# A two-block network on one core: attention heads among late projections, a two-pass last key tile, a new recurrence order, and the closing norm in columns

## Chip, core and metric

The kernel runs on one core of a Trainium2 chip. A core has five engines with an in-order queue each: TensorE (PE in the profile; its weight loads are PEld), VectorE (DVE), ScalarE (ACT), GpSimd (POOL) and SyncE (SP, which only issues DMAs here). The metric is the device time of one execution in microseconds (us).

## The reference

A sequence of 512 tokens of width 1024 goes through a first block with two layers and then a second block with gated linear attention. The change touches the first layer's recurrence, the second layer's attention and the norm at the very end:

```python
# layer 0: recurrence
gate, xr = split(h @ w_in, 2); gate = gelu(gate)
xc = conv_b + sum(xpad[:, k:k + S] * conv_w[k] for k in range(4))
r, i = sigmoid(xb @ w_a + b_a), sigmoid(xb @ w_x + b_x)      # blocks of 256
log_a = -8 * r * softplus(-lam);  a = exp(log_a)
u = sqrt(-expm1(2 * log_a)) * (i * xc)
y = (scan of h = a * h + u) * gate;  return y @ w_out

# layer 1: attention over keys that an index picks
q, c, qi, ki, wi = split(h @ w_in);  c = rms_norm(c)
q_lat = q @ w_uk * ATT_SCALE                                  # 16 heads
score = sum(wi * relu(qi @ ki))          # 8 index heads, causal
idx = top_k(score, 128)
logits = q_lat @ c_sel + rel_bias[t5_bucket(dist)]
p = softmax(logits);  o = (p @ c_sel) @ w_uv;  return o @ w_o

# end of the second block
return x * rsqrt(mean(x * x) + EPS) * norm_final
```

## The kernel before

**Products.** Activations and weights lie feature by token, 128 features on the partitions. Each fp32 operand is split into a rounded part and the rest (`h`/`l`, type fp32r), and a product is made as three: h·h, l·h, h·l. `group()` issues these three for each k tile (L349 to L351), and `lin()` makes a 128x512 output tile from 8 k tiles, so from 24 products. The other products on TensorE are transposes and some in fp32 or bf16.

**Weights.** `Weights` (L222) loads weights in the fixed order of `weight_plan()` (L100), 3 chunks of 128x1024 ahead of use: a DMA on SP's queue, a copy to `wh` on ScalarE (L252), and the rest `wl` on VectorE or, for some keys, on GpSimd (L253).

**Jobs.** Work is written as jobs, lists of stages. `run(jobs)` issues, in step n, stage 0 of job n and then the later stages of the jobs before it. Each engine's instructions stand in its queue in about this order; the framework's scheduler moves some by their readiness. PSUM has 8 buffers that are taken in turn.

**Layer 0.** Eight jobs `conv_job` project `xr` (24 products each) and convolve it: eviction on VectorE, taps, split on ScalarE and VectorE (`split`, L362). Four jobs `recur_job` (key "ax") make gates from two blocks `xr` each: 4 small groups of products, tanh (L568), exp, tanh, square root (L590) on ScalarE, whose function tables are loaded anew when the function's set changes, and factors and a scan on VectorE. Eight `rgate_job` project the gate (24 products), apply gelu and multiply by the scan. The order is xr0 to xr3; xr4, xr5, ax0; xr6, xr7, ax1; gates 0, 1, ax2; gates 2, 3, ax3; gates 4 to 7. `bias_job` (L624) makes the table of the relative biases by one product, copies it (`biasrow`, L639, VectorE) and stores it in DRAM; it stands after gates 0, 1 and ax2. Then `rout` projects back, four tiles together and then four more.

**Attention.** 8 index heads score the keys of query tiles 1 to 3 (`index_job`, relu L784, sum L793). `select()` (L801) finds the 128 largest of each row: 16 rounds of `max` (L811) and `match_replace` (L812) on VectorE for each of the three tiles, and a mask after each (L814). Rounds are issued by `more()` in the heads' jobs, two in each of the first 16. There are 32 head jobs (`head_job`, L903), pair 0 for query tiles 0 and 1 (masks 0 and 1), then pair 1 for tiles 2 and 3 (masks 2 and 3), 16 each. A head loads its bias rows, makes logits (L927 to L929), the softmax (minimum with bias on VectorE L938, exponential L941 on ScalarE, reciprocal of the sums L943, scaling on GpSimd L946), transposes (L958), copies and splits the transposed probabilities (`pTh` L961, `pTl` L962, `pTf` L966), and multiplies by the values (L978, L979, and L981 in fp32 for the last key tile). Of every two heads one output pair is put together: two copies `olo` on ScalarE (L985, L986), two additions on VectorE (L987, L988), and the split (`oh` L993, `ol` L994). The jobs' order is the projections q0 to q7 among the index heads, 8 key tiles, the values among the first four heads, then the other heads.

**The end.** The last layer's tiles are made in a left and a right half of 256 tokens (`last_job`, addition L1453; squares `sq`, L1429 and L1433). `norm_job` (L1460) makes, per half, the sum over all features with two fp32 products with a matrix of ones (`tot`, L1467), root and reciprocal on 128x256 (L1471, L1472), and four products `fin` (L1477) with a DMA each (L1478).

Of the kernel before, what the change touches and what calls it, by code (L numbers as in the profile page):

```python
# [11 lines left out]
F32 = mybir.dt.float32  # L12
# [86 lines left out]

def weight_plan():  # L100

    plan = []
    for step in range(8):
        plan += [("xr" if step < 4 else "rgate", 2 * step % 8 + i) for i in range(2)]
        if 2 <= step <= 5:
            plan += [("ax", step - 2)]
    plan += [("routk", kk) for kk in range(4)] + [("rout", j) for j in range(4, 8)]
    plan += mlp_plan(0, HID_GROUPS, False)
    plan += [("att", j) for j in (0, 1, 2, 3, 4, 6, 7, 8, 9, 5, 10, 11, 12, 13)] + [("uk",), ("uv",)]
# [113 lines left out]
class Weights:  # L223
# [3 lines left out]
    def __init__(self, nc, wall, pool, ahead):  # L227
        self.nc, self.wall, self.pool, self.ahead = nc, wall, pool, ahead
        self.plan = weight_plan()
        self.done = []  # L230
        self.off = 0
        self.at = 0

# [14 lines left out]
    def _split(self, key, st, h, l, a, b):  # L248


        eng = self.nc.gpsimd if key[0] in ("att", "uk", "uv", "lr", "k", "dec") or key == ("q", 0) else self.nc.vector
# [3 lines left out]
    def fetch(self, n):  # L255
        while len(self.done) < min(len(self.plan), n):
# [23 lines left out]
def build(ctx, tc, xT, wall, par, relb, onehot, edges, out):  # L280
# [364 lines left out]
    for step in range(8):  # L645
        jobs += [(conv_job if step < 4 else rgate_job)(2 * step % 8 + i) for i in range(2)]
        if 2 <= step <= 5:
            jobs.append(recur_job(step - 2))
        if step == 4:
            jobs.append(bias_job())  # L650
# [20 lines left out]
    run([residual_job(j, lambda j=j: rout(j), nxt) for j in range(KD)])  # L671
# [98 lines left out]
    def index_job(i, h):  # L770
# [10 lines left out]
        def relu():  # L781

            d = st["d"] = T(name="dots") if on_pool else st["ps"]
# [119 lines left out]
    def head_job(pair, h):  # L903
# [5 lines left out]
        def loads():  # L909
# [38 lines left out]
        def transpose():  # L948
            probs = st["p"]
            st["pT"] = []  # L950
            for k0 in range(0, nfull + 1, 2):
# [7 lines left out]
                nf = 256 if k0 + 1 == nfull else 512  # L959
# [3 lines left out]
                pf = None  # L963
                if nf == 256:
                    pf = T(name="pTf")
                    act(pf[:, :P], ps[:, 256:256 + P], AF.Copy)  # L966
                st["pT"].append((ph, pl, pf))

        def values():
# [4 lines left out]
            for kt in range(nfull + 1):  # L974
                ph, pl, pf = st["pT"][kt // 2]
                if kt < nfull:
                    c = slice((kt % 2) * 256, (kt % 2) * 256 + 256)
                    PE.matmul(osl, value(kt, h), ph[:, c], start=kt == 0, stop=False)  # L978
                    PE.matmul(osl, value(kt, h), pl[:, c], start=False, stop=False)  # L979
                else:  # L980
                    PE.matmul(osl[:, P:], value(kt, h).bitcast(F32), pf[:, :P], start=False, stop=True)  # L981
# [3 lines left out]
            act(lo[0:64, :256], ops[64:128, 0:256], AF.Copy)  # L985
            act(lo[64:128, :256], ops[0:64, 256:512], AF.Copy)  # L986
            V.tensor_add(reverse(lo[0:64, 256:512]), blocks(lo[0:64, :256]), blocks(ops[0:64, 0:256]))  # L987
            V.tensor_add(reverse(lo[64:128, 256:512]), blocks(lo[64:128, :256]), blocks(ops[64:128, 256:512]))  # L988
# [4 lines left out]
            act(oh_[:, c], lo[:, 256:512], AF.Copy)  # L993
            G.tensor_sub(ol_[:, c], lo[:, 256:512], oh_[:, c].bitcast(F32))  # L994
# [11 lines left out]
    for j in range(1, 8):  # L1006
        jobs.append(q_job(j))
        if j == 3:
# [3 lines left out]
        if 3 <= j <= 5:  # L1012
            jobs.append([lambda: None, lambda j=j: copies(0, j - 3)])
        if 5 <= j <= 6:
            jobs.append([lambda: None, lambda j=j: queries(0, j - 5)])
    heads = [head_job(pair, h) for pair in range(2) for h in range(16)]

# [532 lines left out]
```

## Time and profile before

| | |
|---|---|
| median of 3 runs (lowest to highest) | 1905.28 us (1903.79 to 1905.71) |
| the profiled execution's own time | 1903.61 us |
| its span in the trace | 1901.8 us |
| busy: TensorE, VectorE, ScalarE, GpSimd | 1848.7, 1020.3, 813.4, 181.7 us |
| idle TensorE in the span | 53 us |

The trace gives every instruction's start and busy time. The start of one product to the start of the next is TensorE's pace; a product's busy time is longer, since products overlap in the pipeline. A number in brackets behind an instruction is the idle time before it on its engine, and who ended it. The granted clock is a share of TensorE's full 2.4 GHz: at 0.5 it runs at 1.2 GHz.

### The profile page before, as it was taken

What the parts mean: (1) busy time and instruction counts of PE and PEld (TensorE: products, weight loads), DVE (VectorE), ACT (ScalarE), POOL (GpSimd) and SP (SyncE); (2) the same over time, 40 slices, a digit from 0 to 9 for tenths busy, and PEclk for the clock granted to TensorE, in tenths of its full rate; (3) what the DMA queues carried; (4) which work ended last, traced back from release to release, by engine and by line L of the source; (5) the groups of instructions that cost most, each with busy time, mean ns of one, the idle gap of its engine ahead of it and who ended that gap; (6) DMA issues with size and microseconds to landing.
All of it is one profiled execution on the core that took longest, in us unless ns stands there. A gap on an engine that the chain in (4) does not pass through costs nothing.

```text
span 1901.8 us, 21845 instructions
## 1 busy us (share of the span) xinstructions
PE 1848.7 (97%) x8434; PEld 1526.0 (80%) x8434; DVE 1020.3 (54%) x1512; ACT 813.4 (43%) x1271; POOL 181.7 (10%) x194
## 2 busy tenths in 40 slices
PE   8989999999999679999999999999999999999997
PEld 6868888888878468888888888888888888888886
DVE  7886543344349956654244445735584554344345
ACT  6784432333244577443234445446543333132223
POOL 0000000000155264000000014211000000000000
PEclk9999999999999899999999999999999999999998
DMA  5222222222222530322222222231122222222221
GB/s 197 84 86 92 100 98 91 100 100 96 93 100 90 146 89 21 111 93 96 100 100 92 97 100 86 92 111 45 67 89 100 100 89 100 100 95 94 100 80 53
DMA packets 61000, 179.36 MB, mean 94 GB/s; under 512 B 7696, under 2 KB 18144, under 8 KB 60896
## 3 DMA queue, kind: packets, MB, share of 16 engines
q1 hardware_dynamic: 60752, 177.97, 27.6%
q8 instruction: 66, 1.08, 0.2%
q14 instruction: 38, 0.31, 0.0%
q10 hardware_dynamic: 144, 0.00, 0.0%
HBM read 168.48 MB, written 2.12 MB: 90 GB/s over the span
## 4 chain that ended last, share of the span: by engine, by line
PE 63%; DVE 4%; ACT 2%; issue 1%; DMA 0%; POOL 0%; SPq 0%; DVEq 0%; ACTq 0%
PE ps L349 14%; PE ps L351 13%; PE ps L350 13%; PE dn L350 5%; PE dn L351 5%; PE dn L349 5%; PE o L1319 1%; DVE score L812 1%; PE v L1225 1%; PE v L1224 1%; PE v L1226 1%; DVE top L811 1%; ACT probs L941 1%; PE kv L1293 1%; PE tot L376 0%
## 5 line engine op out<-in xcount | busy, mean ns | idle before, releaser
L252 ACT ACTIVATE wh<-wst 128x1024 fp32r<-128x1024 f32 (+2 forms) x314 | 328.2, 1047 | 910.3 <-PE ps L350 358.7
L349 PE MATMUL ps<-xh,wh 128*128 128x512 f32 x1376 | 542.5, 394 | 6.4 <-DVE biasrow L639 4.6
L351 PE MATMUL ps<-xh,wl 128*128 128x512 f32 x1376 | 536.6, 390 | 0.0
L350 PE MATMUL ps<-xl,wh 128*128 128x512 f32 x1376 | 536.5, 390 | 0.0
L253 DVE TENSOR_TENSOR wl<-wst,wh 128x1024 fp32r<-128x1024 f32 (+2 forms) x291 | 352.4, 1212 | 224.3 <-ACT wh L252 197.2
L349 PEld LDWEIGHTS ps<-xh,wh 128*128 128x128 f32 x1376 | 259.3, 188 | 62.8 <-issue 7.2
L350 PEld LDWEIGHTS ps<-xl,wh 128*128 128x128 f32 x1376 | 259.3, 188 | 56.3 <-issue 2.4
L351 PEld LDWEIGHTS ps<-xh,wl 128*128 128x128 f32 x1376 | 259.1, 188 | 54.1
L349 PE MATMUL dn<-h,wh 128*128 128x512 f32 (+1 forms) x712 | 271.7, 382 | 0.0
L350 PE MATMUL dn<-l,wh 128*128 128x512 f32 (+1 forms) x712 | 271.7, 382 | 0.0
L351 PE MATMUL dn<-h,wl 128*128 128x512 f32 (+1 forms) x712 | 271.7, 382 | 0.0
L350 PEld LDWEIGHTS dn<-l,wh 128*128 128x128 f32 x712 | 133.8, 188 | 26.0
L349 PEld LDWEIGHTS dn<-h,wh 128*128 128x128 f32 x712 | 133.8, 188 | 26.0
L351 PEld LDWEIGHTS dn<-h,wl 128*128 128x128 f32 x712 | 133.8, 188 | 25.8
L253 POOL TENSOR_TENSOR wl<-wst,wh 128x1024 fp32r<-128x1024 f32 x23 | 55.2, 2405 | 934.7 <-ACT wh L252 934.5
L422 DVE TENSOR_TENSOR x<-x,dn 128x512 f32<-128x512 f32 x48 | 33.0, 687 | 170.8 <-PE dn L351 170.8
L453 DVE SCALAR_TENSOR_TENSOR relu<-ps,std 128x512 f32<-128x512 f32 x64 | 44.2, 691 | 146.7 <-PE ps L351 146.6
L349 PE MATMUL ps<-h,wh 128*128 128x512 f32 x200 | 78.7, 396 | 5.5 <-ACT h L362 3.5
L350 PE MATMUL ps<-l,wh 128*128 128x512 f32 x200 | 77.8, 389 | 0.0
L351 PE MATMUL ps<-h,wl 128*128 128x512 f32 x200 | 77.8, 389 | 0.0
L349 PEld LDWEIGHTS ps<-h,wh 128*128 128x128 f32 x200 | 37.9, 190 | 15.1 <-ACT h L362 4.0
L1497 DVE TENSOR_TENSOR u<-ps,std 128x512 f32<-128x512 f32 x22 | 15.2, 690 | 62.5 <-PE ps L351 62.5
(315 smaller groups left out, 2129.2 us busy)
## 6 DMA issues: line engine op xcount, KB each, us to landing
wst<-wall SPq DMA_DIRECT2D x300, 512.0 KB, 3.2
btile<-biasdram SPq DMA_DIRECT2D x32, 128.0 KB, 3.0
qd<-qq SPq DMA_DIRECT2D x64, 64.0 KB, 2.1
wst<-wall SPq DMA_DIRECT2D x8, 384.0 KB, 3.0
x<-xT SPq DMA_DIRECT2D x8, 256.0 KB, 4.9
out_dram<-fin SPq DMA_DIRECT2D x8, 256.0 KB, 2.3
wst<-wall SPq DMA_DIRECT2D x6, 256.0 KB, 5.0
kto<-kth SPq DMA_DIRECT2D x8, 128.0 KB, 2.7
```

The lines of the kernel that those rows point to most:

```text
L252: self.nc.scalar.activation(h[:, a:b], st[:, a:b], AF.Copy)
L253: eng.tensor_sub(l[:, a:b], st[:, a:b], h[:, a:b].bitcast(F32))
L349: PE.matmul(ps, wh, xh, start=i == 0, stop=False)
L350: PE.matmul(ps, wh, xl, start=False, stop=False)
L351: PE.matmul(ps, wl, xh, start=False, stop=i == n - 1)
L422: V.tensor_add(xs[j], xs[j], st["ps"])
L453: stt(t, st["ps"], 0.0, feed.r, op0=ALU.max, op1=ALU.mult)
L811: V.max(top, acc[:, :w])
L812: V.match_replace(acc[:, :w], top, acc[:, :w], MARK)
L941: act(s[:, :w], s[:, :w], AF.Exp, scale=-1.0, bias=nm, accum_out=sums[:, a:a + 1])
L1224: PE.matmul(st["ps"][i], xh, hk, start=kt == 0, stop=False)
L1225: PE.matmul(st["ps"][i], xh, lk, start=False, stop=False)
```

## The change

Layer 0's jobs and weights get one order, `LAYER0`: seven projections, then the first recurrence, and the rest with one or two gate projections between recurrences. `bias_job` moves behind the first four output tiles. In attention the weights of q6 and q7 come after `uk` and `uv`; the output projection's weights ("wo") are held back until a job `further` behind head 9, and their `wl` is made on GpSimd; the first heads stand among q6, q7, the key tiles and the values; a head fetches the copies 3 pairs ahead and the queries 2 ahead; index head jobs of tile 1 write their relu to SBUF. The last key tile's probabilities are split with the others, and multiplied in two rounded passes. An output pair has one copy of 128x512. At the end the sums over the features are made as columns (128x2), root and reciprocal work on these, and two products with the identity spread them back into PSUM (`r`); the left half's norm is one job earlier.

```diff
+LAYER0 = ([("xr", j) for j in range(7)] + [("ax", 0), ("xr", 7), ("rgate", 0), ("ax", 1), ("rgate", 1), ("rgate", 2)]
+          + [("ax", 2), ("rgate", 3), ("rgate", 4), ("ax", 3)] + [("rgate", j) for j in range(5, 8)])
...
-    plan += [("att", j) for j in (0, 1, 2, 3, 4, 6, 7, 8, 9, 5, 10, 11, 12, 13)] + [("uk",), ("uv",)]
+    plan += [("att", j) for j in (0, 1, 2, 3, 4, 6, 7, 8, 9, 5, 10, 11)] + [("uk",), ("uv",), ("att", 12), ("att", 13)]
...
+        self.limit = self.plan.index(("wo", 0))
...
-        eng = self.nc.gpsimd if key[0] in ("att", "uk", "uv", "lr", "k", "dec") or key == ("q", 0) else self.nc.vector
+        eng = self.nc.gpsimd if key[0] in ("att", "uk", "uv", "wo", "lr", "k", "dec") or key == ("q", 0) else self.nc.vector
...
-        while len(self.done) < min(len(self.plan), n):
+        while len(self.done) < min(self.limit, n):
...
+    jobs += [{"xr": conv_job, "ax": recur_job, "rgate": rgate_job}[n](j) for n, j in LAYER0]
     run(jobs)
...
-    run([residual_job(j, lambda j=j: rout(j), nxt) for j in range(KD)])
+    jobs = [residual_job(j, lambda j=j: rout(j), nxt) for j in range(KD)]
+    run(jobs[:4] + [bias_job()] + jobs[4:])
...
-            d = st["d"] = T(name="dots") if on_pool else st["ps"]
+            d = st["d"] = T(name="dots") if on_pool or i == 1 else st["ps"]
...
-            if e == 0 and 1 <= n < 14:
-                copies((n + 2) // 8, (n + 2) % 8)
-            if e == 1 and 1 <= n < 15:
-                queries((n + 1) // 8, (n + 1) % 8)
+            if e == 0 and n + 3 < 16:
+                copies((n + 3) // 8, (n + 3) % 8)
+            if e == 1 and n + 2 < 16:
+                queries((n + 2) // 8, (n + 2) % 8)
...
-                nf = 256 if k0 + 1 == nfull else 512
+                nf = 384 if k0 + 1 == nfull else 512
...
-                pf = None
-                if nf == 256:
-                    pf = T(name="pTf")
-                    act(pf[:, :P], ps[:, 256:256 + P], AF.Copy)
-                st["pT"].append((ph, pl, pf))
+                st["pT"].append((ph, pl))
...
-                    PE.matmul(osl[:, P:], value(kt, h).bitcast(F32), pf[:, :P], start=False, stop=True)
+                ph, pl = st["pT"][kt // 2]
+                c = slice((kt % 2) * 256, (kt % 2) * 256 + (256 if kt < nfull else P))
+                dst = osl if kt < nfull else osl[:, P:]
+                PE.matmul(dst, value(kt, h), ph[:, c], start=kt == 0, stop=False)
+                PE.matmul(dst, value(kt, h), pl[:, c], start=False, stop=kt == nfull)
...
-            act(lo[0:64, :256], ops[64:128, 0:256], AF.Copy)
-            act(lo[64:128, :256], ops[0:64, 256:512], AF.Copy)
+            act(lo, ops, AF.Copy)
+            os_ = T(name="os")
+            V.tensor_add(reverse(os_[0:64, :256]), blocks(lo[64:128, 0:256]), blocks(ops[0:64, 0:256]))
+            V.tensor_add(reverse(os_[64:128, :256]), blocks(lo[0:64, 256:512]), blocks(ops[64:128, 256:512]))
...
-    for j in range(1, 8):
+    for j in range(1, 6):
         jobs.append(q_job(j))
...
+    jobs += kts[:2] + vals[:2] + [heads[0], q_job(6), heads[1], q_job(7)]
+    for i in range(2, 8, 2):
+        jobs += [heads[i // 2 + 1]] + kts[i:i + 2] + vals[i:i + 2]
+
+    def further():
+        W.limit = len(W.plan)
+        W.fetch(W.at + W.ahead)
+
+    run(jobs + heads[5:10] + [[further]] + heads[10:])
...
-            ps = st["ps"] = PS("tot")[:, :w]
-            for i in range(2):
-                PE.matmul(ps, ones, acc2[i][:, c], start=i == 0, stop=i == 1)
+            ps = st["ps"] = PS("tot")
+            for n in range(w // P):
+                cols = slice(c.start + n * P, c.start + (n + 1) * P)
+                for i in range(2):
+                    PE.matmul(ps[:, n:n + 1], acc2[i][:, cols], ones[:, 0:1], start=i == 0, stop=i == 1)
...
-            r = st["r"] = T(name="std")[:, :w]
-            act(r, st["ps"], AF.Sqrt, scale=1.0 / D, bias=eps_t)
-            V.reciprocal(r, r)
+            col = small(w // P, "rstd")
+            act(col, st["ps"][:, :w // P], AF.Sqrt, scale=1.0 / D, bias=eps_t)
+            V.reciprocal(col, col)
+            st["r"] = PS("r")[:, :w]
+            for n in range(w // P):
+                PE.matmul(st["r"][:, n * P:(n + 1) * P], col[:, n:n + 1].to_broadcast([P, P]), ident, start=True, stop=True)
...
-    jobs.insert(-2, norm_left[:3])
+    jobs.insert(-3, norm_left[:3])
```

TensorE's queue where the first recurrence's products (`ps_485` to `ps_506` from the split block `h_460` before, `ps_527` to `ps_548` after) follow the projections of `xr`; before:

```order
L350 MATMUL ps_435<-xl_189,wh_308 128x512
L351 MATMUL ps_435<-xh_188,wl_309 128x512
L349 MATMUL ps_485<-h_460,wh_340 128x512
L349 MATMUL ps_492<-h_460,wh_340 128x512
L349 MATMUL ps_499<-h_460,wh_340 128x512
L349 MATMUL ps_506<-h_460,wh_340 128x512
L349 MATMUL ps_530<-xh_148,wh_382 128x512
L350 MATMUL ps_530<-xl_149,wh_382 128x512
```

and now:

```order
L351 MATMUL ps_485<-xh_188,wh_340 128x512
L352 MATMUL ps_485<-xl_189,wh_340 128x512
L353 MATMUL ps_485<-xh_188,wl_341 128x512
L351 MATMUL ps_527<-h_460,wh_382 128x512
L351 MATMUL ps_534<-h_460,wh_382 128x512
L351 MATMUL ps_541<-h_460,wh_382 128x512
L351 MATMUL ps_548<-h_460,wh_382 128x512
L351 MATMUL ps_572<-xh_148,wh_430 128x512
```

One more projection, xr6 (now `ps_485`; `ps_435` before was xr5), stands ahead of the recurrence's first products.

VectorE's queue around the third mask (`mask3`); `probs` and `negmax` are a head's softmax minima, `sums` its reciprocals, `olo` and `os` an output pair's additions, `top` and `score` the selection's rounds. Before:

```order
L938 ISA probs_4996,negmax_4997<-logit_4976,btile_3784 128x128
L938 ISA negmax_4997 128x1
L938 ISA probs_5000,negmax_5001<-logit_4976,btile_3784 128x256
L938 ISA negmax_5001 128x1
L814 TENSOR_SCALAR mask3_3775<-score_4301 128x512
L943 RECIPROCAL sums_4964<-sums_4964 128x2
L987 TENSOR_TENSOR olo_5022<-olo_5022,o_4920 64x2x128
L988 TENSOR_TENSOR olo_5022<-olo_5022,o_4920 64x2x128
L943 RECIPROCAL sums_4995<-sums_4995 128x2
```

and now:

```order
L979 TENSOR_TENSOR os_5177<-olo_5175,o_5004 64x2x128
L980 TENSOR_TENSOR os_5177<-olo_5175,o_5004 64x2x128
L809 MAX top_5155<-score_4314 128x8
L810 MATCH_REPLACE score_4314<-top_5155,score_4314 128x512
L960 TENSOR_TENSOR pTl_5189<-pT_5184,pTh_5188 128x384
L936 ISA probs_5193,negmax_5194<-logit_5158,btile_3784 128x128
L936 ISA negmax_5194 128x1
L936 ISA probs_5197,negmax_5198<-logit_5158,btile_3784 128x256
L936 ISA negmax_5198 128x1
L812 TENSOR_SCALAR mask3_3775<-score_4314 128x512
L960 TENSOR_TENSOR pTl_5226<-pT_5221,pTh_5225 128x384
```

Ahead of the mask stood 7 heads' minima and one output pair; now stand 11 heads' minima, 8 splits `pTl` and 3 output pairs, and the last round of selection follows the third pair.

VectorE's queue at the end (`x` are the additions of the last layer, right half; `fin` the left half's closing products, then `sq` the right half's squares). Before:

```order
L1472 RECIPROCAL std_14255<-std_14255 128x256
L1453 TENSOR_TENSOR x_83<-x_83,dn_14232 128x256
L1477 TENSOR_TENSOR fin_14096<-fin_14096,std_14255 128x512
L1477 TENSOR_TENSOR fin_14032<-fin_14032,std_14255 128x512
L1477 TENSOR_TENSOR fin_14148<-fin_14148,std_14255 128x512
L1477 TENSOR_TENSOR fin_14197<-fin_14197,std_14255 128x512
L1433 TENSOR_TENSOR sq_14030<-sq_14030,sq_14282 128x256
L1453 TENSOR_TENSOR x_84<-x_84,dn_14258 128x256
L1429 TENSOR_TENSOR sq_14288<-x_84 128x256
L1472 RECIPROCAL std_14298<-std_14298 128x256
```

and now:

```order
L1473 RECIPROCAL rstd_14209<-rstd_14209 128x2
L1451 TENSOR_TENSOR x_82<-x_82,dn_14185 128x256
L1481 TENSOR_TENSOR fin_14072<-fin_14072,r_14212 128x512
L1481 TENSOR_TENSOR fin_14008<-fin_14008,r_14212 128x512
L1481 TENSOR_TENSOR fin_14124<-fin_14124,r_14212 128x512
L1481 TENSOR_TENSOR fin_14173<-fin_14173,r_14212 128x512
L1431 TENSOR_TENSOR sq_14006<-sq_14006,sq_14258 128x256
L1451 TENSOR_TENSOR x_83<-x_83,dn_14215 128x256
L1431 TENSOR_TENSOR sq_14006<-sq_14006,sq_14263 128x256
L1451 TENSOR_TENSOR x_84<-x_84,dn_14239 128x256
L1427 TENSOR_TENSOR sq_14269<-x_84 128x256
L1473 RECIPROCAL rstd_14281<-rstd_14281 128x2
```

The left half's four closing products stood after the addition of `x_83` and just before that of `x_84`; now they stand before both.

## Rows read from the trace of the kernel before

**Rows 1.** The page: busy time of each engine, share of the span, instructions.
```profile
PE 1848.7 (97%) x8434; PEld 1526.0 (80%) x8434; DVE 1020.3 (54%) x1512; ACT 813.4 (43%) x1271; POOL 181.7 (10%) x194
```

**Rows 2.** Busy us (instructions) by stretch; PEclk is the granted clock.
```profile
41.60:121.00 79.40, 69.28 (x293) 55.60 (x293) 67.72 (x93) 63.61 (x87) 0.00 (x0) 0.97 0.23 81
45.10:48.30 3.20, 3.15 (x8) 2.49 (x9) 3.20 (x6) 1.97 (x3) 0.00 (x0) 0.51 0.47 164
120.40:124.00 3.60, 3.58 (x10) 2.89 (x11) 3.60 (x6) 3.06 (x4) 0.00 (x0) 0.59 0.29 83
580.00:664.00 84.00, 65.92 (x296) 51.36 (x294) 81.97 (x206) 39.19 (x92) 29.90 (x29) 0.90 0.44 124
664.00:745.00 81.00, 70.05 (x435) 57.54 (x435) 55.51 (x192) 68.59 (x216) 50.49 (x77) 0.96 0.28 67
```

**Rows 3.** What TensorE waited for, 20 to 145 us: total, times, longest.
```profile
PE ps L349 <- DVE biasrow L639: 4.6, 1, 4.6
PE ps L349 <- ACT h L362: 3.5, 1, 3.5
PE ps L349 <- ACT rg L568: 2.0, 2, 1.1
```

**Rows 4.** Timeline of TensorE, layer 0: start, busy us, instruction, [idle before, releaser].
```profile
24.24 0.39 PE L349 MATMUL ps<-xh,wh 128*128 128x512 f32 x1
24.47 0.39 PE L350 MATMUL ps<-xl,wh 128*128 128x512 f32 x1
```

**Rows 5.** Timeline of VectorE around the third mask and the pairs' additions.
```profile
661.87 0.42 DVE L938 CUSTOM_DVE_ANT_0 probs<-logit,btile 128x256 f32<-128x256 f32 x1
...
662.21 1.43 DVE L814 TENSOR_SCALAR mask<-score 128x512 bf16<-128x512 f32 x1
...
663.64 0.39 DVE L987 TENSOR_TENSOR olo<-olo,o 64x256 f32<-64x256 f32 x1
...
667.72 0.17 DVE L943 RECIPROCAL sums<-sums 128x2 f32<-128x2 f32 x1 [1.42 <-ACT probs L941]
...
678.34 0.41 DVE L987 TENSOR_TENSOR olo<-olo,o 64x256 f32<-64x256 f32 x1 [0.62 <-ACT olo L986]
```

**Rows 6.** Timeline of ScalarE around a function table's load in layer 0.
```profile
91.31 1.28 ACT L590 ACT_TABLE_LOAD   x1
92.60 0.63 ACT L590 ACTIVATE rg<-rg 128x512 f32<-128x512 f32 x1
```

**Rows 7.** Groups by shape, 555 to 760 us: busy, mean ns, idle before.
```profile
L962 DVE TENSOR_TENSOR pTl<-pT,pTh 128x256 fp32r<-128x256 f32 x32 | 13.5, 421 | 5.0 <-ACT pTh L961 3.0 <-POOL probs L946 0.9
...
L253 DVE TENSOR_TENSOR wl<-wst,wh 128x1024 fp32r<-128x1024 f32 x4 | 5.2, 1292 | 0.0
...
L966 ACT ACTIVATE pTf<-pT 128x128 f32<-128x128 f32 x32 | 8.8, 276 | 9.9 <-DVE pTl L962 9.2 <-POOL ol L994 0.6
```

**Rows 8.** Timeline of TensorE in the values of pair 1.
```profile
714.82 0.28 PE L978 MATMUL o<-pTh,vv 128*128 128x256 f32 x1
714.94 0.28 PE L979 MATMUL o<-pTl,vv 128*128 128x256 f32 x1
...
715.82 0.39 PE L981 MATMUL o<-pTf,vv 128*128 128x128 f32 x2
716.04 0.38 PE L927 MATMUL logit<-mask,identb 128*128 128x512 bf16 x1
```

**Rows 9.** Timeline of TensorE and VectorE at the end.
```profile
1888.54 0.28 PE L351 MATMUL dn<-h,wl 128*128 128x256 f32 x1
...
1888.73 2.48 DVE L1477 TENSOR_TENSOR fin<-fin,std 128x512 f32<-128x512 f32 x4
...
1891.47 0.41 DVE L1453 TENSOR_TENSOR x<-x,dn 128x256 f32<-128x256 f32 x1
...
1894.22 1.75 DVE L1472 RECIPROCAL std<-std 128x256 f32<-128x256 f32 x1 [1.88 <-ACT std L1471]
```

**Rows 10.** What TensorE waited for, 620 to 745 us: the longest entry.
```profile
PE pT L958 <- POOL probs L946: 9.8, 4, 8.0
```

More of the change, by code (lines that the diff above doesn't have):

```diff
@@ L97, in mlp_plan @@
     return plan
+LAYER0 = ([("xr", j) for j in range(7)] + [("ax", 0), ("xr", 7), ("rgate", 0), ("ax", 1), ("rgate", 1), ("rgate", 2)]
+          + [("ax", 2), ("rgate", 3), ("rgate", 4), ("ax", 3)] + [("rgate", j) for j in range(5, 8)])
 def weight_plan():
[L102 to L106, printed above, removed]
+    plan = list(LAYER0)
     plan += [("routk", kk) for kk in range(4)] + [("rout", j) for j in range(4, 8)]
     plan += mlp_plan(0, HID_GROUPS, False)
-    plan += [("att", j) for j in (0, 1, 2, 3, 4, 6, 7, 8, 9, 5, 10, 11, 12, 13)] + [("uk",), ("uv",)]
+    plan += [("att", j) for j in (0, 1, 2, 3, 4, 6, 7, 8, 9, 5, 10, 11)] + [("uk",), ("uv",), ("att", 12), ("att", 13)]
     plan += [("wo", j) for j in range(8)]
@@ L644, in build @@
     jobs = [[lambda: None, softplus]]
[L645 to L650, printed above, removed]
+    jobs += [{"xr": conv_job, "ax": recur_job, "rgate": rgate_job}[n](j) for n, j in LAYER0]
     run(jobs)
@@ L974, in values @@
             for kt in range(nfull + 1):
[L975 to L980, printed above, removed]
-                    PE.matmul(osl[:, P:], value(kt, h).bitcast(F32), pf[:, :P], start=False, stop=True)
+                ph, pl = st["pT"][kt // 2]
[3 more added lines that the diff above has]
+                PE.matmul(dst, value(kt, h), pl[:, c], start=False, stop=kt == nfull)
             if e == 0:
@@ L992, in values @@
             c = slice(256 * pair, 256 * pair + 256)
-            act(oh_[:, c], lo[:, 256:512], AF.Copy)
-            G.tensor_sub(ol_[:, c], lo[:, 256:512], oh_[:, c].bitcast(F32))
+            act(oh_[:, c], os_[:, :256], AF.Copy)
+            G.tensor_sub(ol_[:, c], os_[:, :256], oh_[:, c].bitcast(F32))
         def more():
@@ L1005, in build @@
     jobs += [index_job(1, h) for h in range(8)]
-    for j in range(1, 8):
+    for j in range(1, 6):
         jobs.append(q_job(j))
+        if 3 <= j <= 5:
+            jobs.append([lambda: None, lambda j=j: copies(0, j - 3)])
+        if 4 <= j <= 5:
+            jobs.append([lambda: None, lambda: None, lambda j=j: queries(0, j - 4)])
         if j == 3:
@@ L1011, in build @@
             jobs += [index_job(2 + (j - 1) // 2, 4 * ((j - 1) % 2) + h) for h in range(4)]
[L1012 to L1015, printed above, removed]
     heads = [head_job(pair, h) for pair in range(2) for h in range(16)]
+    kts = [kt_job(j) for j in range(8)]
     vals = [v_job(kt, n) for kt, n in ((0, 0), (1, 0), (0, 1), (1, 1), (2, 0), (3, 0), (2, 1), (3, 1))]
-    first = []
-    for i in range(4):
-        first += [heads[i], vals[2 * i], vals[2 * i + 1]]
-    run(jobs + [kt_job(j) for j in range(8)] + first + heads[4:])
+    jobs += kts[:2] + vals[:2] + [heads[0], q_job(6), heads[1], q_job(7)]
[5 more added lines that the diff above has]
+    run(jobs + heads[5:10] + [[further]] + heads[10:])
     nxt = Feed("g_mlp1")
```

2 lines of the change are left out of this document (removed).

## The prediction

> **What bounds the kernel now.** I read first the busy shares: TensorE works 97% of the span [rows 1], so a change that leaves its products alone can win no more than its idle time, some 53 us, and what the products lose at a lower clock. Then the table by stretches, to find where that idle time lies in the stages that the change touches. In layer 0, from 41.60 to 121.00 us, TensorE stands 10.1 us (79.40 less 69.28), while VectorE has 67.72 us of work and ScalarE 63.61 [rows 2]. In attention, from 580 to 745 us, it stands 18.1 us of the first 84 and 10.9 of the next 81. VectorE is busy 81.97 of the 84 and only 55.51 of the 81 [rows 2]: the first stretch is VectorE's, the second nobody's. So two questions follow: which waits are the 10.1 us, and what makes VectorE full in one stretch and half idle in the next.
>
> The waits of layer 0 name three: 4.6 us for the bias row's copy, 3.5 us for the first split of a convolved block, and 2.0 for gates, together the window's 10.1 [rows 3]. Each long one leaves a cold stretch behind it: the granted clock is 0.51 for 3.20 us and 0.59 for 3.60 us [rows 2], so TensorE loses 3.20 x 0.49 = 1.57 us and 3.60 x 0.41 = 1.48 us there. A product of 512 columns follows the next after 0.23 us at the full clock [rows 4].
>
> In attention the third mask ends the selection at 662.21 [rows 5]: rounds of maximum and replacement on VectorE feed it, and the heads of pair 1 can't start before it. After it the pairs of pair 0 still unfinished are done, and then pair 1.
>
> **Layer 0, the order.** The seven projections now stand ahead of the first recurrence, so the block's split has 24 more products, 24 x 0.23 = 5.5 us of TensorE's work, to finish behind. That covers the 3.5 us wait and its 1.57 us of cold clock. One gate projection instead of two stands between some recurrences; a round there is 72 products, 16.5 us of TensorE. The bias product goes behind the first 28 products of the output projection, and its copy waits in VectorE's queue behind nothing that TensorE needs: 4.6 and 1.48 us go. With the 2.0 us for gates the most that can be had is 10.1 + 3.1 = 13.2 us. It costs one more function table on ScalarE, 1.28 us [rows 6]. If all is had, the window is 66.2 us, and must hold ScalarE's 63.61 + 1.28 = 64.9 us and VectorE's 67.7 us, of which the last scan and products can trail into the output projection. That is the edge, so I take 12 us, between 6 (only bias) and 13.2.
>
> The trace shows a table's load as one instruction of 1.28 us, and the work behind it starts 0.01 us after [rows 6]. The Trainium skill, page "ScalarE: Activation LUTs", section "What ACT_TABLE_LOAD costs", puts a drain of about 1.38 us beside the load, some 2.66 us a switch. By that, the eight loads in this window and the new one would hide up to 9 x 1.38 = 12.4 us more, and the gain here would be about 2 us. The row disagrees, and the sum goes by the row.
>
> **Attention, the order.** The first heads now start among the late q, k and v products. By the queue's order, VectorE does eleven heads' softmax minima ahead of the third mask instead of seven, and three output pairs instead of one; the fourth comes shortly after. So two pairs more are finished when pair 1 may begin. In the trace the second pair's additions start at 663.64 and the fourth's at 678.34 [rows 5]: 14.7 us. Not all of that is won, since the same instructions now stand before the mask, on the engine that is full there. The wider of a head's two minima takes 0.34 us to the next instruction (661.87 to 662.21), the narrower less, some 0.54 together [rows 5]: 2.2 for four heads. Four reciprocals of 0.17 and four additions of 0.4 are 0.7 and 1.6 [rows 5]; four splits of transposed probabilities 4 x 0.42 = 1.7 [rows 7]; that the eight splits there become half as wide again costs at most 8 x 0.21, and I estimate 0.9. Against that, four subtractions of the output projection's weights, 5.2 us [rows 7], leave VectorE for GpSimd; I count 4.6 of it, since busy times overlap those of the next instruction by a tenth or more. That nets 2.5 us. A split, two minima and a reciprocal of the fourth pair stay behind the mask, 1.4. 14.7 - 2.5 - 1.4 = 10.8 us.
>
> Two corrections. ScalarE loses a copy of 0.28 us for each head and chunk [rows 7], gets wider ones, and does one output copy for two: about 0.2 us for each of the remaining 12 pairs, where it is busy 68.59 of 81 us [rows 2]: +2. And heads in VectorE's in-order queue make it wait: today 2.03 us idle in the 84 [rows 2] over seven heads, 0.3 a head, so 3 us for eleven. Sum 10.8 + 2 - 3 = 10 us. The low end is 2, where VectorE waits for the heads longer; the high end 18, as VectorE's idle time over both stretches, 27.5 us [rows 2], is the most that any order could give and a third of it lies behind the last minima of a head.
>
> Index head 1's relu into SBUF instead of over its own PSUM frees a buffer and adds no instruction: nothing. The copies and queries of the heads are DMAs and splits moved one head or two earlier; SP's queue has fewer weight loads ahead of them, since the output weights are held back. Nothing, covered by the head before; the output weights come back with heads still to run.
>
> **Last key tile.** One fp32 product of 128 columns for each head and tile gives way to two rounded ones. The trace has the fp32 one at 0.22 us, two records together from 715.82 to 716.04 [rows 8]. It doesn't show a rounded one of 128 columns; the bounds are 0.06 each by the slope from 512 columns (0.23) to 256 (0.12) [rows 4, 8], so 0.13 for two, and 0.22 each if it is as slow per column as fp32. That is -0.09 to +0.22 a head. TensorE sets the end only for the 16 heads of pair 1: a gain of 1.4 to a loss of 3.5 us. I take 0, since the nearest row, 256 columns at 0.12, speaks for the lower half and the weight load behind each product for the other.
>
> **Closing norm.** The last product starts at 1888.54 and takes 0.28, but VectorE is in the left half's four closing products from 1888.73 for 2.48 us, and so the last addition waits until 1891.47 [rows 9]. In the new order these stand ahead of the last two additions, behind the left half's norm, which is one job earlier: the last addition can start at 1888.9, -2.6 us. Then the norm's root and reciprocal work on two columns instead of 256: the reciprocal of 128x256 takes 1.75 us [rows 9], one of 128x2 0.17 [rows 5]. The sums as columns are tiny products, and the spreading back costs two products of 128 columns, 0.22 each [rows 8] and a hop to TensorE and back. I take -1.7 in all. The left half's spreading now stands in TensorE's queue among the last products, and its chain of root and reciprocal may outlast the nine products ahead of it (9 x 0.12 = 1.1 us): +0.8. Sum: 3.5 us, between 1 and 5.
>
> **Sum.** 12 + 10 + 0 + 3.5 = 25.5 us. The profiled execution took 1903.61 us, 1.7 below the median of the three; 1903.6 - 25.5 = 1878.1, and 1.7 more is 1879.8: 1880.
>
> **Rivals.** *VectorE's queue gives the attention back* (1890). The early heads' chains go from VectorE to ScalarE, GpSimd, TensorE and back; each return stands in order among selection rounds. For it speaks a row where VectorE waits 1.42 us for ScalarE's exponential before a reciprocal [rows 5]; if each of eleven heads costs 1.2 us, not 0.3, the 10 us are gone. Against it: rounds stand between most of these steps, and VectorE idles only 2 us of 84 with seven heads [rows 2].
>
> *ScalarE bounds the recurrence* (1886 to 1890). With 64.9 us in 66.2 any wait of its own is lost; if only the bias wait and its cold clock go, layer 0 gives 6 us. With the hidden drain of the sentence above it would give 2. Against it the 1.28 us row [rows 6].
>
> *Slower: an early head stops the selection for its whole chain* (1921). TensorE's longest wait for GpSimd's scaled probabilities is 8.0 us [rows 10]; if the transposed probabilities' split is queued on VectorE ahead of rounds and half of such a wait, 4 us, comes with each of eleven heads, 44 us are lost against the 3 I have counted: 1880 + 41 = 1921. It decides from (25.5 + 3 + 3.8) / 11 = 2.9 us a head. Against it: four stages lie between softmax and transposition in a head's job, and rounds stand there.
>
> *The waits only move* (1904). TensorE waits the same for other reasons, since VectorE and ScalarE are both at 80 to 85% in layer 0 and VectorE is full before the mask. For it speaks how near the new window is to VectorE's work; against it that the bias wait and the last addition's have nothing behind them to take their place.
>
> **How the numbers follow.** Forecast 0.70, the first rival 0.10, the second 0.07, the slower one 0.08, no change 0.05. A difference of 0.2%, 3.8 us, is about what can be told from none here. Faster holds the first three: 0.87; same 0.05; slower 0.08. Range: all high ends give 37.7 us, so 1868; all low ends 5.5 us, so 1900, but they don't fall together: 1896, which covers the first two rivals.
>
> **What would show it.** In the changed profile: no wait for the bias row and none over 1 us for a split in layer 0, and no clock near 0.5 between 40 and 125 us; layer 0's output projection beginning some 10 to 12 us earlier. The third mask at about the same time after layer 0's gain, within 4 us, and the fourth pair's additions within 2 us of it. No VectorE idle over 10 us before the mask. At the end 11 us or less from the last product to the end instead of 13.3. The forecast is wrong if VectorE idles more than 1 us per early head, if ScalarE is over 97% busy in layer 0, or if pair 1's pace per pair grows.

## The result

The changed kernel took 1878.38 us (median of 4 runs, 1878.08 to 1880.16), the kernel before 1904.53 us beside it: 26.2 us less, a ratio of 0.9864 with an interval of 0.9847 to 0.9881. The forecast was 1880. That the sum came out so near is partly luck: its terms did not, as the traces and the runs with one part alone show.

The profiled execution took 1878.08 us, its span is 1876.1. TensorE's busy time on the page of the changed kernel, which answers to [rows 1]:

```profile
PE 1838.0 (98%) x8450; PEld 1522.8 (81%) x8450; DVE 1020.1 (54%) x1504; ACT 807.4 (43%) x1224; POOL 201.4 (11%) x202
```

Where the time went is read from the sums over the features that open each norm, the same product in both kernels. Timeline of TensorE before, at four of them (norm of the first network, of attention, of the second network, and of the second block's network):

```profile
187.19 0.59 PE L376 MATMUL tot<-sq,ones 128*128 128x512 f32 x1
...
536.23 0.59 PE L376 MATMUL tot<-sq,ones 128*128 128x512 f32 x1
...
802.01 0.59 PE L376 MATMUL tot<-sq,ones 128*128 128x512 f32 x1
...
1548.71 0.59 PE L376 MATMUL tot<-sq,ones 128*128 128x512 f32 x1
```

and in the changed kernel:

```profile
179.81 0.59 PE L378 MATMUL tot<-sq,ones 128*128 128x512 f32 x1
...
528.85 0.59 PE L378 MATMUL tot<-sq,ones 128*128 128x512 f32 x1
...
778.99 0.59 PE L378 MATMUL tot<-sq,ones 128*128 128x512 f32 x1
...
1525.68 0.59 PE L378 MATMUL tot<-sq,ones 128*128 128x512 f32 x1
```

Layer 0 is 7.4 us shorter, of which 0.9 is the first product's earlier start (6.77 us for 7.71). The network behind it is the same (349.04 us in both). Attention takes 250.1 us instead of 265.8, 15.6 less. The middle is the same to 0.01, and from the last of these sums to the end of the span it is 350.4 instead of 353.1, 2.7 less. 7.4 + 15.6 + 2.7 = 25.7, the difference of the spans.

**Layer 0.** The bias row's wait and the first split's are gone, as forecast. The waits for the gates' tanh have grown from 2.0 us to 5.4, in two, with a stretch at about half the clock behind the longer one. Waits of TensorE from 20 to 145 us, against [rows 3], and two stretches, against [rows 2]:

```profile
PE ps L351 <- ACT rg L570: 5.4, 2, 4.0
```

```profile
41.60:121.00 79.40, 73.98 (x318) 60.41 (x318) 67.34 (x93) 62.77 (x85) 0.00 (x0) 0.98 0.25 85
87.24:90.50 3.26, 3.26 (x8) 2.59 (x9) 2.26 (x4) 3.23 (x5) 0.00 (x0) 0.51 0.03 5
```

The longer one can be followed through three queues (timelines of TensorE, VectorE and ScalarE):

```profile
87.24 0.77 PE L351 MATMUL ps<-h,wh 128*128 128x512 f32 x1 [3.99 <-ACT rg L570]
```

```profile
84.03 1.22 DVE L600 TENSOR_TENSOR_SCAN hs<-q,ig 128x512 f32<-128x512 f32 x1
85.16 0.73 DVE L546 SCALAR_TENSOR_TENSOR xc<-xr,params,xc 128x511 f32<-128x511 f32 x1
```

```profile
85.98 0.63 ACT L364 ACTIVATE h<-xc 128x512 fp32r<-128x512 f32 x1 [2.73 <-DVE xc L546]
86.52 0.67 ACT L570 ACTIVATE rg<-ps,half_b 128x512 f32<-128x512 f32 x1
```

TensorE waits for a PSUM buffer that the tanh reads. The tanh stands in ScalarE's queue behind the split of the eighth projection, that waits for its last tap, and the tap stands in VectorE's queue behind a scan.

**The third mask** comes 132.1 us after the attention norm's sum (before: 126.0), and the fourth pair's additions right behind it. Timeline of VectorE, against [rows 5]:

```profile
660.91 0.48 DVE L812 TENSOR_SCALAR mask<-score 128x512 bf16<-128x512 f32 x1
...
662.51 0.42 DVE L979 TENSOR_TENSOR os<-olo,o 64x256 f32<-64x256 f32 x1
```

**The end.** TensorE and VectorE, against [rows 9]: the last addition starts 0.32 us after the last product's start instead of 2.93, and the reciprocal costs 0.17 instead of 1.75.

```profile
1866.35 0.28 PE L353 MATMUL dn<-h,wl 128*128 128x256 f32 x1
...
1868.99 1.19 PE L1476 MATMUL r<-ident,rstd 128*128 128x128 f32 x4 [0.55 <-DVE rstd L1473]
```

```profile
1866.67 0.42 DVE L1451 TENSOR_TENSOR x<-x,dn 128x256 f32<-128x256 f32 x1 [0.25 <-PE dn L353]
...
1868.77 0.17 DVE L1473 RECIPROCAL rstd<-rstd 128x2 f32<-128x2 f32 x1 [1.22 <-ACT rstd L1472]
```

### The profile page after: what moved, and what is told of

The parts are those of the page before. It is cut to its first block, busy times and chain, and to the rows that moved or that the text cites. A ratio compares the mean times of both kernels' runs of the same rounds, so it can differ in the third digit from the quotient of the medians.

```text
span 1876.1 us, 21800 instructions
## 1 busy us (share of the span) xinstructions
PE 1838.0 (98%) x8450; PEld 1522.8 (81%) x8450; DVE 1020.1 (54%) x1504; ACT 807.4 (43%) x1224; POOL 201.4 (11%) x202
## 4 chain that ended last, share of the span: by engine, by line
PE 91%; DVE 5%; ACT 2%; DMA 1%; issue 1%; POOL 0%; SPq 0%; DVEq 0%; ACTq 0%; POOLq 0%
PE ps L351 19%; PE ps L353 19%; PE ps L352 19%; PE dn L352 8%; PE dn L353 8%; PE dn L351 8%; DVE score L810 1%; PE o L1317 1%; DVE top L809 1%; PE ps L522 1%; PE v L1222 1%; PE v L1223 1%; PE v L1224 1%; DVE score L791 1%; PE kv L1291 1%
## 5 line engine op out<-in xcount | busy, mean ns | idle before, releaser
L255 DVE TENSOR_TENSOR wl<-wst,wh 128x1024 fp32r<-128x1024 f32 (+2 forms) x283 | 342.6, 1211 | 221.6 <-ACT wh L254 194.8
L255 POOL TENSOR_TENSOR wl<-wst,wh 128x1024 fp32r<-128x1024 f32 x31 | 75.8, 2452 | 916.6 <-ACT wh L254 916.4
L353 PEld LDWEIGHTS dn<-h,wl 128*128 128x128 f32 x712 | 133.8, 188 | 25.7
```

The source lines that it names most:

```text
L255: eng.tensor_sub(l[:, a:b], st[:, a:b], h[:, a:b].bitcast(F32))
L353: PE.matmul(ps, wl, xh, start=False, stop=i == n - 1)
```

## Experiments: each part alone

The first theory, from the two traces: layer 0 gave 7.4 us, the end 2.7, and in attention the order gave what lies up to the fourth pair's additions (8.4 us), the last tile and the pair's copy what lies behind (7.2). The rival for attention: the order gave both.

**bias_only** moves the bias product and nothing else.

```diff
-        if step == 4:
-            jobs.append(bias_job())
...
+    run(jobs[:4] + [bias_job()] + jobs[4:])
```

> The kernel before with the bias product alone moved behind the first four output tiles. Theory (the wait was only the copy's place in VectorE's queue): the 4.6 us wait and the 1.48 us of cold clock behind it go, 6.1 us, so some 1898.4 against 1904.5. Rival (the recurrence's own chain would have made TensorE wait there a little later): 0 to 2 us gained, 1902.5 to 1904.5, with a new wait for gates or splits between 100 and 125 us.

Measured: 1897.05 us against 1903.84, 6.8 us less (ratio 0.9962, 0.9949 to 0.9975). The wait was only the copy's place in the queue. In its profiled run the first network's norm comes 4.3 us earlier (182.88 us); another 2.0 lie in attention, which has the same code as before (263.8 us for 265.8), so not all of the 6.8 is the bias product's. The other waits of layer 0 stay as they were; the first two entries:

```profile
PE ps L349 <- ACT h L362: 3.6, 1, 3.6
PE ps L349 <- ACT rg L568: 1.7, 2, 0.9
```

**layer0_only** adds the new order of layer 0 to that.

```diff
+LAYER0 = ([("xr", j) for j in range(7)] + [("ax", 0), ("xr", 7), ("rgate", 0), ("ax", 1), ("rgate", 1), ("rgate", 2)]
+          + [("ax", 2), ("rgate", 3), ("rgate", 4), ("ax", 3)] + [("rgate", j) for j in range(5, 8)])
...
+    run(jobs[:4] + [bias_job()] + jobs[4:])
```

> The kernel before with the new order of layer 0 and the bias product moved, nothing else. Theory (layer 0 gave 7.4 us in the changed kernel, and does so alone): 1897.1 against 1904.5, with the waits of 1.4 and 4.0 us for the gates' tanh as in the changed kernel. So the new order is worth only about 1.3 us beyond the bias product's move. Rival (the attention part has a share in it, by an earlier start of its weights): 1899 or more.

Measured: 1894.53 us, 9.3 less (0.9954, 0.9939 to 0.9969). By the medians the order is worth some 2.5 us beyond the bias product, but the two intervals overlap. The traces place it better. The first product's start differs by up to 1.7 us between profiles (6.05 to 7.71 us), whatever the kernel, so it is taken off. From the first product to the first network's norm it is then 179.5 us before, and 181.0 to 181.6 in norm_only, last_tile_only and att_order_only, which have the same layer 0; 176.0 in bias_only; and 173.0 to 175.0 in six traces with the new order. So the order gives about 1 to 3 us beyond the bias product, though it takes away a wait of 3.5 us with its cold clock. One and the same layer 0 differs by 2 us, and with the new order that lies in the stretch at half the clock behind one and the same wait of 4.0 us: 3.3 us in the changed kernel's profile, 5.8 (87.4 to 93.2 us, 0.50) in that of layer0_only, the slowest of its four runs.

**att_order_only** is the attention's order with the weights' order, without the last tile and the pair's copy.

```diff
+    jobs += kts[:2] + vals[:2] + [heads[0], q_job(6), heads[1], q_job(7)]
+    for i in range(2, 8, 2):
+        jobs += [heads[i // 2 + 1]] + kts[i:i + 2] + vals[i:i + 2]
...
+    run(jobs + heads[5:10] + [[further]] + heads[10:])
```

> The kernel before with the heads' order, the weights' order, the held back output weights and the earlier copies, but with the last key tile in fp32 and two copies for a pair. Theory (the order finishes two pairs more ahead of the third mask, and nothing else): the fourth pair's additions come about 2 us after the mask instead of 16.1, the mask some 6 us later, pairs 4 to 16 take their 75.9 us as before: 14.5 - 6.1 - 1.4 = 7 us, 1897.5. Rival (the order also makes pair 1's rounds shorter): 15 us, 1889.5, with pairs 4 to 16 in 67 to 69 us.

Measured: 1900.46 us, only 3.4 less (0.998, 0.9971 to 0.9989). In its trace attention takes 261.8 us; in the four traces with the old attention (before, bias_only, layer0_only, norm_only) it takes 263.8 to 266.2. The mask comes 2.6 us later, but two pairs, not three, stand before it, and the fourth comes 9.7 us behind it. Timeline of VectorE (second pair, mask, fourth pair):

```profile
650.49 0.39 DVE L988 TENSOR_TENSOR olo<-olo,o 64x256 f32<-64x256 f32 x1
...
666.42 0.41 DVE L815 TENSOR_SCALAR mask<-score 128x512 bf16<-128x512 f32 x1
...
676.12 0.41 DVE L988 TENSOR_TENSOR olo<-olo,o 64x256 f32<-64x256 f32 x1 [0.70 <-POOL probs L947]
```

**last_tile_only** is the other part of attention.

```diff
-                    PE.matmul(osl[:, P:], value(kt, h).bitcast(F32), pf[:, :P], start=False, stop=True)
+                PE.matmul(dst, value(kt, h), ph[:, c], start=kt == 0, stop=False)
+                PE.matmul(dst, value(kt, h), pl[:, c], start=False, stop=kt == nfull)
...
-            act(lo[0:64, :256], ops[64:128, 0:256], AF.Copy)
-            act(lo[64:128, :256], ops[0:64, 256:512], AF.Copy)
+            act(lo, ops, AF.Copy)
```

> The kernel before with the last key tile in two rounded passes and one copy for an output pair. Theory (the shorter chain from the values to the pair's additions gave pairs 4 to 16 their 8.6 us): 6 to 8.6 us gained, 1896 to 1898.5, with VectorE's wait for the copy olo much shorter. Rival (the order did it): within 1.5 us of the kernel before, 1903 to 1905.

Measured: 1893.57 us, 10.3 less (0.9945, 0.9928 to 0.9961), more than the theory gave it and three times what the order gives alone. **no_last_tile**, the changed kernel with the same lines as before, says it from the other side:

```diff
+                    PE.matmul(osl[:, P:], value(kt, h).bitcast(F32), pf[:, :P], start=False, stop=True)
...
+            act(lo[0:64, :256], ops[64:128, 0:256], AF.Copy)
+            act(lo[64:128, :256], ops[0:64, 256:512], AF.Copy)
```

> The changed kernel with the last key tile in fp32 and two copies for an output pair, as before. Theory (these shorten the pairs' rounds): 6 to 8.6 us slower than the changed kernel, 1884.5 to 1887. Rival (the order did it): 1878 to 1880.

Measured: 1889.26 us, 10.9 slower than the changed kernel. From the start of the fourth pair's additions to the sixteenth's, before, order alone, last tile alone, changed (columns as in [rows 2]):

```profile
678.34:754.24 75.90, 67.87 (x406) 56.39 (x407) 50.69 (x159) 60.95 (x181) 40.86 (x60) 0.96 0.21 48
```

```profile
676.10:751.90 75.80, 69.33 (x419) 57.37 (x418) 51.98 (x164) 63.11 (x189) 41.54 (x61) 0.96 0.20 49
```

```profile
678.60:743.70 65.10, 61.20 (x407) 52.25 (x407) 53.13 (x160) 55.91 (x150) 41.47 (x61) 1.00 0.26 59
```

```profile
662.50:729.85 67.35, 61.00 (x412) 52.76 (x413) 54.11 (x165) 57.09 (x153) 42.36 (x63) 1.00 0.25 59
```

The order does nothing for this stretch. Six of the products that stood in it before stand behind it in the changed kernel (1.4 us, found again between the last pair and the next norm), so 7.2 of its 8.6 us are gain.

**norm_only** is the closing norm.

```diff
+                    PE.matmul(ps[:, n:n + 1], acc2[i][:, cols], ones[:, 0:1], start=i == 0, stop=i == 1)
...
-    jobs.insert(-2, norm_left[:3])
+    jobs.insert(-3, norm_left[:3])
```

> The kernel before with the closing norm alone changed (columns, spreading back, left half one job earlier). Theory: 2.7 us as between the two traces, 1901.8 against 1904.5. Rival (the end was shortened by the earlier parts, for example by the weights' timing): under 1 us.

Measured: 1901.55 us against 1904.34, 2.8 less (0.9986, 0.9977 to 0.9995), as between the traces.

The four parts alone give 9.3 + 3.4 + 10.3 + 2.8 = 25.8 us, together 26.2. Each of the four is known to some 2 to 3 us only, so the agreement to 0.4 is more than the runs can show.

## Experiments: why the last tile is worth 10 us

**no_rounded** and **old_pair_copy** undo one half each in the changed kernel: the fp32 product with its copy `pTf`, or the two copies of a pair.

```diff
+                    pf = T(name="pTf")
+                    act(pf[:, :P], ps[:, 256:256 + P], AF.Copy)
...
+                    PE.matmul(osl[:, P:], value(kt, h).bitcast(F32), pf[:, :P], start=False, stop=True)
```

> The changed kernel with the last key tile back in fp32 (its own copy pTf on ScalarE, which waits for VectorE's split, and one fp32 product), but with the one copy for an output pair. Together the two cost 10.9 us. Theory (both lie in ScalarE's queue in the pairs' rounds; the copy pTf with its wait is the larger one): 5 to 8 us slower than the changed kernel, 1883.5 to 1886.5. Rival (the pair's copy alone, which frees the output's PSUM buffer): 0 to 2 us, 1878.5 to 1880.5.

```diff
-            act(lo, ops, AF.Copy)
+            act(lo[0:64, :256], ops[64:128, 0:256], AF.Copy)
+            act(lo[64:128, :256], ops[0:64, 256:512], AF.Copy)
```

> The changed kernel with two copies of 64x256 for an output pair instead of one of 128x512, the last key tile still in rounded passes. Theory: 3 to 5 us slower than the changed kernel, 1881.5 to 1883.5, VectorE waiting longer for the copy olo. Rival (the pair's copy is the cause of all): 9 to 11 us, 1887.5 to 1889.5; other rival (nothing): 1878 to 1879.

Measured: 1883.99 us, 5.6 slower than the changed kernel, and 1881.18 us, 2.8 slower. The first is clear. The second is near what can be told from none (1879.31 to 1881.63 us against 1878.08 to 1880.16), though attention is 2.7 us longer in its trace too; and whether both together (10.9) are more than their sum of 8.4 can't be told. **copy_before_split** keeps the fp32 product and the copy, but issues the copy ahead of VectorE's split, which reads the same PSUM tile:

```diff
                 act(ph[:, :nf], ps[:, :nf], AF.Copy)
-                V.tensor_sub(pl[:, :nf], ps[:, :nf], ph[:, :nf].bitcast(F32))
                 pf = None
                 if nf == 256:
                     pf = T(name="pTf")
                     act(pf[:, :P], ps[:, 256:256 + P], AF.Copy)
+                V.tensor_sub(pl[:, :nf], ps[:, :nf], ph[:, :nf].bitcast(F32))
```

> The changed kernel with the last key tile in fp32, as in no_rounded, but with the copy pTf issued ahead of VectorE's split of the same PSUM tile, so that ScalarE doesn't wait for VectorE before it. Theory (most of the 5.6 us that no_rounded lost is ScalarE's wait before that copy, 6.0 us in 12 waits between 665 and 740 us): 3 to 5 us of it come back, 1879 to 1881. Rival (it is the copy's own 0.28 us and the fp32 product): 1883 to 1885.

Measured: 1879.99 us. 4.0 of the 5.6 us come back by that order alone (in the traces attention falls from 256.3 to 251.3 us); 1.6, no more than the noise, are left for the copy's own time and the product. So the larger part was a wait, not work. What ScalarE waited for before this copy, in no_rounded and in copy_before_split from 665 to 740 us, and in the kernel before from 678.34 to 754.24 us:

```profile
ACT pTf L964 <- DVE pTl L960: 6.0, 12, 0.8
```

```profile
ACT pTf L963 <- DVE pTl L964: 0.3, 1, 0.3
```

```profile
ACT pTf L966 <- DVE pTl L962: 5.7, 12, 0.9
```

The chain goes on in the same stretch before: a late ScalarE copies the pair's output late, VectorE's additions wait for it, and TensorE for the PSUM buffers that the additions free. First VectorE's waits, then TensorE's:

```profile
DVE olo L987 <- ACT olo L986: 13.0, 10, 4.6
```

```profile
PE pT L958 <- DVE olo L988: 3.4, 2, 1.9
PE logit L927 <- DVE olo L988: 3.2, 2, 1.8
```

With the last tile alone changed, VectorE's wait is 5.6 us, and no wait of TensorE for an addition is above 0.4 us; the clock, 0.96 in that stretch before, is 1.00.

```profile
DVE os L981 <- ACT olo L979: 5.6, 3, 4.3
```

In the trace before, two stretches at half the clock (688 to 690 us at 0.51, 708 to 710 at 0.50) follow two such waits for additions each, of 1.4 to 1.9 us. But the chain is not the whole. TensorE's idle time in the stretch is 8.0 us before, 6.5 with the order alone, 3.9 with the last tile alone and 6.4 in the changed kernel, where other waits stand in place of those for the additions. Of the 8.6 us between before and changed, 6.9 are busy time (67.87 to 61.00): 1.4 are the six products, some 3 the clock (an estimate: 0.04 of 75.9 us), some 1.2 the last tile's products (an estimate: 23 heads at 0.22 less 0.17), and 1.3 are left without a cause.

The rounded product itself, in the changed kernel's timeline of TensorE, takes 0.06 us for 128 columns, the lower bound of the forecast, and 0.17 for both to the next instruction, against 0.22 in fp32 [rows 8], the commonest of the 32 there:

```profile
698.73 0.22 PE L972 MATMUL o<-pTh,vv 128*128 128x128 f32 x1
698.79 0.28 PE L973 MATMUL o<-pTl,vv 128*128 128x128 f32 x1
698.90 0.30 PE L956 MATMUL pT<-ident,probs 128*128 128x128 f32 x1
```

## Experiments: what bounds layer 0 now

Three versions of the changed kernel were to take the 4.0 us wait away. **split7_later** sets the split of the eighth projection a stage later, behind the tanh:

```diff
-        return [mm] + [lambda: None] * max(0, 2 - j) + [evict, taps, out_]
+        return [mm] + [lambda: None] * max(0, 2 - j) + [evict, taps] + [lambda: None] * (j == 7) + [out_]
```

> The changed kernel with one stage more ahead of the split of the eighth projection (xr7), so that the second recurrence's tanh no longer stands behind it in ScalarE's queue. Theory (the 4.0 us wait of TensorE at 83 us is that split, which waits for VectorE's taps): the wait and its 1.6 us of cold clock go, 4 to 5.6 us faster than the changed kernel, 1873 to 1874.5. Rival (VectorE's and ScalarE's work bounds layer 0, so the wait comes back later in it): 1877 to 1879, with waits of the same sum between 85 and 125 us.

**pairs_of_gates** goes back to two gates between recurrences, with xr6 still ahead:

```diff
+LAYER0 = ([("xr", j) for j in range(7)] + [("ax", 0), ("xr", 7), ("ax", 1), ("rgate", 0), ("rgate", 1)]
+          + [("ax", 2), ("rgate", 2), ("rgate", 3), ("ax", 3)] + [("rgate", j) for j in range(4, 8)])
```

> The changed kernel with layer 0 in the old pattern (xr7, second recurrence, two gates, third, two gates, fourth), but with xr6 still ahead of the first recurrence. Theory (only the first wait of 3.5 us and the bias product's were worth anything, the alternation with gates brought the 4.0 us wait): waits of about 1 us each at the second and third recurrence, 3 to 5 us faster than the changed kernel, 1873.5 to 1875.5. Rival (ScalarE's work bounds any order): within 1 us of 1878.4.

Measured: 1878.91 and 1877.82 us, both the same as the changed kernel within the measurement. The theories fall: the wait of 4.0 us is 0.64 in the first and gone in the second, but others take its place. TensorE's waits from 20 to 145 us, in this order:

```profile
PE ps L351 <- ACT rg L570: 4.2, 3, 2.2
```

```profile
PE ps L351 <- ACT rg L570: 5.9, 2, 5.0
```

In all three orders TensorE waits 4 to 6 us, always for the gates' tanh. **layer0_wl_gpsimd** asked whether VectorE's load is behind it, by giving its subtractions `wl` of layer 0 to GpSimd, which does nothing there:

```diff
-        eng = self.nc.gpsimd if key[0] in ("att", "uk", "uv", "wo", "lr", "k", "dec") or key == ("q", 0) else self.nc.vector
+        eng = self.nc.gpsimd if key[0] in ("ax", "rgate", "att", "uk", "uv", "wo", "lr", "k", "dec") or key == ("q", 0) or key[0] == "xr" and key[1] > 3 else self.nc.vector
```

> The changed kernel with the weights' second parts wl of layer 0 (xr4 to xr7, ax, rgate: 16 of 1.22 us) made on GpSimd, which does nothing there, instead of VectorE. Theory (VectorE's queue is what keeps the taps, the split and so the gates' tanh back at 83 us): the waits of 1.4 and 4.0 us and 1.6 us of cold clock go, 5 to 7 us faster than the changed kernel, 1871.5 to 1873.5. Rival (ScalarE's 63 us of 72 bound the stage, or GpSimd takes VectorE's time): within 1.5 us, 1877 to 1880.

Measured: 1890.29 us, 11.9 slower than the changed kernel. VectorE has fewer instructions, and some of those take longer, most of all the taps of 128x510 (those of 128x511 rise from 0.746 to 1.007 us, those of 128x509 stay at 0.74). Taps of 128x510 in the changed kernel and here, from 41.6 to 121 us:

```profile
L546 DVE SCALAR_TENSOR_TENSOR xc<-xr,params,xc 128x510 f32<-128x510 f32 x8 | 5.8, 747 | 0.1
```

```profile
L546 DVE SCALAR_TENSOR_TENSOR xc<-xr,params,xc 128x510 f32<-128x510 f32 x8 | 15.8, 1982 | 0.1
```

ScalarE then waits 24.8 us for taps from 40 to 125 us, and TensorE for ScalarE. The question it was to settle stays open: that run shows that a slower VectorE costs time here, not that a faster one would gain any.

```profile
ACT h L364 <- DVE xc L546: 24.8, 6, 5.9
```

## Why the prediction came out, and where it did not

- **Layer 0, forecast 12, measured 7.4 in the trace** (9.3 by medians alone). The bias product's term, 6.1, fits what bias_only gave (6.8 by medians, 4.3 up to the norm in its trace). The first split's wait went, as worked out. The step that failed is "if all is had": the waits for gates, 2.0 us, were counted as gone and became 5.4, with 3.26 us at 0.51 of the clock behind them, 1.6 us. 10.1 - 5.4 + 3.05 - 1.6 = 6.2, near the trace's 7.4, or 6.4 from the first product on. The edge that the text named (66.2 us for 64.9 of ScalarE and 67.7 of VectorE) was the place; only the bounds held, and the value should have been nearer the low one. Of the rival "ScalarE bounds the recurrence" this is half: always the tanh, but which of the two engines is behind it is not settled. The one more table load came (nine in the window for eight), each at 1.28 us, and the trace shows no drain beside it.
- **Attention up to the fourth pair, forecast 7.8 (10.8 - 3), measured 8.4.** The two pairs, the 5.5 us that the mask was to come later (6.1) and the 1.4 us from mask to fourth pair (1.6 us) stand in the trace of the changed kernel. But the term was given to the order, and the order alone brings 3.9 us there in its trace, since it finishes one pair less ahead of the mask: the heads' rounds must be short enough as well. The first rival (VectorE's queue gives it back) is not what happened either: the mask was only 2.6 us later.
- **Attention behind the fourth pair, forecast 2 + 0, measured 7.2.** The mis-sized step. The copies' busy time (0.2 us a pair) and the product's price were weighed, and the waits in front of them were not, though [rows 7] print them: 9.2 us idle before the copy `pTf`, released by VectorE's split. One engine's wait in an in-order queue, then the next engine's, then a PSUM buffer, then the clock: 7.2 us where the text had counted 2. That ScalarE's wait starts it is shown by copy_before_split; how the 7.2 divide along the chain is only estimated. The product's 0 was off by less, 0.05 us a head in these rows.
- **The closing norm, forecast 3.5, measured 2.7.** The last addition came 2.6 us earlier as worked out, the reciprocal is 0.17, and from the last product's start to the end it is 9.8 us instead of 13.3: 3.5 where the text's two gains gave 4.3. So the spreading back over TensorE left 0.9 of the 1.7 that was counted. The 0.8 for the left half's products among the others is there.
- **Sum.** 4.6 too much in layer 0, 0.6 and 5.2 too little in attention, 0.8 too much at the end: 0.4 too little in all, against 25.7 by the spans. (The high ends of the range add up to 37.6, not 37.7; the bound is the same.) The time was right because two wrong terms, of nearly the same size, cancelled; that is luck. Of the signs that the text named, the fourth pair's held and the end's; "no clock near 0.5", the output projection 10 to 12 us earlier (it starts at 124.3 us for 132.8, 8.4 earlier) and the mask within 4 us did not. The last could not hold by the text's own sum, which put 2.5 + 3 = 5.5 us ahead of the mask.
- **The slower rival** (selection stopped for each head) did not occur: from 600 us to the mask VectorE waited 2.6 us in three waits, and three pairs stood before it.

## What to carry to other kernels

A row's idle time says more than its busy time where engines wait for each other in a ring: ask who is queued behind a waiting instruction, and price that wait. Two readers of one PSUM tile were kept in the order in which they were written; issuing ScalarE's first gave back 4.0 us of the 5.6 that the fp32 last tile costs here, with no instruction more or less. And after a sum has come out, run each part alone: a right total can hide two wrong terms.

## What was not expected of the hardware

In these rows VectorE's products and differences of two tensors in SBUF stand still when they start while GpSimd works on SBUF. In layer0_wl_gpsimd a split of VectorE (0.69 us in the changed kernel) starts at 79.71 and takes 2.48, to half a microsecond behind GpSimd's end at 81.64:

```profile
79.23 2.41 POOL L255 TENSOR_TENSOR wl<-wst,wh 128x1024 fp32r<-128x1024 f32 x1 [8.93 <-ACT wh L254]
```

```profile
79.71 2.48 DVE L365 TENSOR_TENSOR l<-xc,h 128x512 fp32r<-128x512 f32 x1 [2.07 <-ACT h L364]
```

Two evictions that read PSUM during another of GpSimd's take 1.28 together, as in the changed kernel at 95.57 us, and the SBUF product behind them waits:

```profile
107.88 2.40 POOL L255 TENSOR_TENSOR wl<-wst,wh 128x1024 fp32r<-128x1024 f32 x1 [2.41 <-ACT wh L254]
```

```profile
107.87 1.28 DVE L613 TENSOR_TENSOR gate<-ps,std 128x512 f32<-128x512 f32 x2
109.07 1.77 DVE L589 TENSOR_TENSOR ig<-ig,q 128x512 f32<-128x512 f32 x1
```

The Trainium skill, page "SBUF — State Buffer", section "SBUF: two separate sides", says that of a GpSimd instruction and a VectorE instruction in a two-port mode, or with two SBUF inputs where GpSimd's reads SBUF too, the one that starts first holds a shared port pair for its whole length and the other fully blocks; these rows agree. The mask of the kernel before looks the same, though it reads only one tensor, and the trace doesn't say in which mode it ran: 1.43 us [rows 5], to 0.28 us behind the end of a split of GpSimd's that had begun 0.12 us ahead of it, and 0.48 in the changed kernel, where such a split ended 0.19 us into it. GpSimd's timeline before:

```profile
662.09 1.27 POOL L896 TENSOR_TENSOR qpl<-qd,qph 128x512 fp32r<-128x512 f32 x1
```
